# The feed-forward stage's second matrix in seven half-size products, with weight sums made by accumulating DMAs

## The chip, the core and the metric

The kernel runs on one NeuronCore of a Trainium2 chip. Its time is device microseconds of the whole program, the median of three runs. TensorE (PE) multiplies matrices, ScalarE (ACT), VectorE (DVE) and GpSimd (POOL) work on tiles in SBUF, and SyncE (SP) only issues DMAs.

## The reference, cut to what matters

The program is a model of two blocks on 512 tokens of width 1024 in fp32. Attention layers, a memory and a pooling layer come first; the change leaves them alone. The last stage is a feed-forward network (FFN) and a last norm:

```python
hm = rms_norm(x, g_mlp[l])                                    # (512, 1024)
x = x + jnp.square(jax.nn.relu(hm @ w_up[l])) @ w_down[l]     # (1024, 4096), (4096, 1024)
return rms_norm(x, g_final)
```

`jnp.square(relu(...))` is called ff below. "Up" is the product with `w_up`, "down" the one with `w_down`.

## The kernel before, in words

Every product of fp32 matrices is made of three matmuls of rounded parts (`mm3`, L376 to L378): each operand is split into a high part `hi` (rounded by ACT) and the rest `lo` (a DVE subtraction), and hi·hi, hi·lo and lo·hi are summed in PSUM. Weights come from HBM in slabs of 1 MB (8 x 256 or 4 x 512 columns a partition, tile `wraw`), by DMAs on SP's queue. `split_slab` makes `whi` (ACT, L208) and `wlo` (DVE, L209) of them in four pieces of 512 columns. Two raw slabs and two split slabs are resident at a time.

The program is a list of units, each of which emits one product and may return a "post", the work on its result, which is emitted behind the next unit. `emit` walks the list, and behind each unit it emits pieces of coming splits and the loads of slabs whose buffers are free. So the order of every engine's queue is fixed when the program is built; at run time each engine takes its queue in order and waits on semaphores.

The FFN goes in four chunks of 1024 hidden columns. `up(c)` makes 8 products 128x512 of 24 matmuls each (8 k x 3) from four slabs; its post takes relu (ACT), the square (DVE) and splits it into tiles `ffgh` and `ffgl` (L392, L393), which are double-buffered. `down(c)` goes over two halves of 512 output columns; in each, four blocks of 128 tokens (`tb`) take 24 matmuls 128x512 (8 k x 3) from two slabs; the post adds the PSUM tile to `x` (DVE, L1873). `x` is eight tiles, `xs[tb][half]`. Two products of `up(c+1)` are emitted ahead of `down(c)`, the other six behind it.

In the last down the second half goes block by block, and `last(tb)` is emitted as soon as a block is complete: the sum of squares of its second half (ACT into `junk`, L438), v^-0.5 by a polynomial in small DVE instructions (L442, L443, L402 to L408), the final gain (POOL, L1898), the scaling (ACT L1899 and DVE L1900, one half each) and two DMAs out. The first halves' sums of squares were made before. POOL does nothing else in the FFN but issue the two loads of the final gain (L432).

Of the kernel before, what the change touches and what calls it, by code (L numbers as in the profile page):

```python
# [26 lines left out]
def block_kernel(ctx: ExitStack, tc: tile.TileContext, A: dict, out: bass.AP, stop=None):  # L27
# [40 lines left out]
    class Pool:  # L68
        """a pool opened and closed by units of the program"""
# [50 lines left out]
    def load_constants():  # L120
        """rows of small vectors, to be transposed to columns; the loads are issued a few at a time"""
# [60 lines left out]
    # ---------------------------------------------------------------- weights: slabs of up to 2112 columns a partition  # L182
# [8 lines left out]
    def dma_slab(key):  # L191
# [5 lines left out]
        raws[key] = t  # L197

    def split_slab(key):
        """hi and lo parts of a slab, in pieces to be emitted one after the other"""  # L200
# [42 lines left out]
    def weave(steps, main, lead=0):  # L243
        """(units before, units after) of each step, with main's units (but the first lead) spread evenly between the two"""
        res, m = main[:lead], 0
        main = main[lead:]
        for i, (before, after) in enumerate(steps):
            to = (len(main) * (i + 1)) // len(steps)
            res += before + main[m:to] + after
            m = to  # L250
        return res

    def soft_steps(scores, norms, trans, values, per, deep=1):
        """steps of an attention: scores of step i, normalization of step i-1 and transposes of the step deep before;
        values of a head after its last transposes"""
# [18 lines left out]
    n = {"dma": 0, "split": 0, "freed": 0, "limit": 0, "start": 2, "step": 2}  # L274
    order = []

    def dma_first(i):
        dma_slab(order[i])
        n["dma"] = i + 1

    def emit():
# [6 lines left out]

        todo = []
# [10 lines left out]

        def pump():
            while n["limit"]:
                if n["split"] < min(n["dma"], n["limit"]) and n["split"] - n["freed"] < NB and not todo:
# [4 lines left out]
                elif n["dma"] < len(order) and n["dma"] - n["split"] < NRAW:  # L308
                    dma_slab(order[n["dma"]])
# [8 lines left out]
        def flush():  # L318
            """a slab's next piece, the second parts of posts, the posts; slabs no more needed are freed"""
            while pend:  # L320
# [12 lines left out]
                for k in prog[i][1]:  # L333
                    if last[k] == i:
                        ready.pop(k)
                        n["freed"] += 1
                pump()

        for i, (fn, keys, early, quiet) in enumerate(prog):
# [9 lines left out]
            for k in keys:  # L349
                if k not in ready:  # L350
                    pieces(order[n["split"] - 1])
                    pump()
                assert k in ready, ("slab not resident", k)
# [8 lines left out]
    def rate(start, step):  # L362
        """pieces of a slab that are split at once, and after a product"""
# [9 lines left out]
    # ---------------------------------------------------------------- helpers  # L373
# [24 lines left out]
    def newton(v, n, eng=None):  # L398
        """v ** -0.5 of [128, n]: from the halved exponent, by a polynomial in v y y"""
# [12 lines left out]
        # the same polynomial as a product of two quadratic ones  # L412
# [13 lines left out]
    # ---------------------------------------------------------------- norms  # L426
# [27 lines left out]
    def norm_T(st, tb, h, dst):  # L454
        """half h of a normed block to columns tb of its transpose; dst(h) gives the tiles of that half"""
# [16 lines left out]
    # ---------------------------------------------------------------- products: units  # L472
# [17 lines left out]
    def fm_halves(items, src="xt"):  # L490
        """(key, c0, post): the first 256 tokens of each, then the rest"""
# [15 lines left out]
    def outproj(name, w, row, nk, slots=(0, 1), blockwise=True):  # L507
        """units of x += y w[128 row...] from slots of y, two parts of 128 rows each"""
# [25 lines left out]
    def boundary(op, mid={}, fa=(), fb=(), gain=False):  # L534
        """the last product into x (block by block), its norm and transpose, and units that run meanwhile"""
# [48 lines left out]
    def mem_kv_units(layer, mt):  # L584
        """keys (normed, transposed) and values of the memory attention into S['mk'], S['mv']"""
# [60 lines left out]
    # ---------------------------------------------------------------- softmax over 256 keys  # L646
# [29 lines left out]
    # ---------------------------------------------------------------- memory attention  # L676
# [79 lines left out]
    # ================================================================ block 1, layer A  # L756
# [20 lines left out]
    def keep_mt():  # L777
        """the normed memory, transposed, for the second layer"""
# [92 lines left out]
    def head_units(h):  # L871
        """z, o, v, q, k of a head"""
# [151 lines left out]
    # h3: tile, z (4), o (2), v (2), q (2), k (2)  # L1024
# [67 lines left out]
    # ================================================================ block 1, layer B  # L1092
# [140 lines left out]
    # ---- heads  # L1233
# [158 lines left out]
    def pt_view(i, j):  # L1392
        """block j of the queries against blocks 0..j of the keys, each 384 columns after the last"""
# [31 lines left out]
    # ================================================================ block 2: pooling and differential attention  # L1425
# [162 lines left out]
    def dprep(h):  # L1588
        """q and k of a head, turned"""
# [19 lines left out]
    def dattend(h):  # L1609
        sc, no, tr, pv = [], [], [], []  # L1610
        for j in range(4):
            def f1(j=j):
# [5 lines left out]
                # the two parts take turns: they hold different rows of the array  # L1618
# [15 lines left out]
            def f2(j=j):  # L1634
                # e0 + (-lambda s0 / s1) e1; the factor 1 / s0 is left to the norm
# [59 lines left out]
    def dsteps():  # L1695
        """steps of the four heads: scores of step i, normalization and transposes of step i-1, values of step i-2"""
# [3 lines left out]
        for i in range(21):  # L1700
# [9 lines left out]
            # after the values of a head's last block: the sums, the products, the transposes  # L1710
# [19 lines left out]
    # y of the pooled part has to be used before that of head 0 is written  # L1730
# [22 lines left out]
    # ================================================================ block 2: cross attention  # L1753
# [81 lines left out]
    def open_ff():  # L1835
# [3 lines left out]
        ffp.open()  # L1839

    def up(c):
        res = []
        for s in range(4):
            key = cslab(("up", c, s), w_up, 1024 * c + 256 * s, 256)
            for i in range(2):
                def post(ps, f_=2 * s + i):
                    if f_ == 0:
                        C["ff", c] = pair(ffp.p, [128, 8, 512], "ffg", bufs=2)
                    g = C["ff", c]
                    r = T("r")  # L1850
                    act.activation(out=r, in_=ps, func=AF.Relu)  # L1851
                    dve.tensor_tensor(out=r, in0=r, in1=ps, op=ALU.mult)  # L1852
                    split(g[0][:, f_, :], g[1][:, f_, :], r)

                res.append((key, 128 * i, post))
        return res

    def down(c):
        res = []
        for half in range(2):  # L1860
            for s in range(2):
                key = cslab(("dn", c, half, s), w_down, 512 * half, 512, k0=8 * c + 4 * s, nk=4)
                for tb in range(4):
                    def fn(w, half=half, s=s, tb=tb):
                        g = C["ff", c]
                        if s == 0:
                            C["dn", tb] = bank([128, 512], "dn")
                        ps = C["dn", tb]
                        t = slice(tb * 128, tb * 128 + 128)
# [5 lines left out]
                    res.append(U(fn, key))  # L1875
# [7 lines left out]
    ups = [up(c) for c in range(4)]  # L1883
    uf, ur = fm_halves(ups[0][0:4])
# [88 lines left out]
```

## Time and profile before

| what | value |
|---|---|
| median of three runs | 1642.2 us (1641.59 to 1644.99) |
| profiled execution, span | 1641.7 us, 0.5 us under that median |
| PE busy in the span | 1581.1 us (96%), 8809 matmuls |
| DVE, ACT, POOL busy | 959.0, 684.2, 148.1 us |
| FFN with its last norm | from about 1296 us to the end |

The span is that of one profiled execution. PE's busy time is the sum of what its matmuls take, weight loads (PEld) run beside them. A row of the timeline gives an instruction's start and its own duration, both in us; what lies between the starts of two matmuls divided by the number of steps is called the pitch below.

### The profile page before, as it was taken

To read this page: it belongs to the slowest core of one execution; us is meant where nothing else is said; L and a number is where in the kernel's file an instruction comes from. 1 tells how busy PE (TensorE), PEld (TensorE's weight loads), DVE (VectorE), ACT (ScalarE), POOL (GpSimd) and SP (SyncE) were. 2 spreads that over 40 slices of the span, in tenths; PEclk is the share of its full clock that TensorE was granted. 3 is DMA by queue.
4 is the path that set the end of the run, shared out by engine and by line. 5 is a ranking of instruction groups with operands and counts; after the bars stand their busy time and mean duration, and the time that the engine had idled before them with its cause. 6 is when DMAs were issued, how large, how long until landed. Compare 5 with 4: busy or idle time off the path is not lost.

```text
span 1641.7 us, 22734 instructions
## 1 busy us (share of the span) xinstructions
PE 1581.1 (96%) x8809; PEld 1342.8 (82%) x8809; DVE 959.0 (58%) x1977; ACT 684.2 (42%) x1491; POOL 148.1 (9%) x471
## 2 busy tenths in 40 slices
PE   6999999999999999999989999998999999999997
PEld 6889898988788978778879877777987888888886
DVE  6558647565685563667776657567357543434345
ACT  6344424333464543444554434455334432323232
POOL 4100000000030000111211000012001000000002
PEclk9999999999999999999999999999999999999999
DMA  8322223132242221212415332224221233223221
GB/s 273 129 78 78 78 82 99 52 103 77 103 136 77 71 78 59 67 35 66 155 39 180 98 101 78 78 90 141 78 78 52 78 103 103 90 90 116 90 90 52
DMA packets 126149, 152.65 MB, mean 93 GB/s; under 512 B 7169, under 2 KB 103193, under 8 KB 126041
## 3 DMA queue, kind: packets, MB, share of 16 engines
q1 hardware_dynamic: 123736, 144.63, 27.5%
q0 software_dynamic: 2304, 6.57, 1.4%
q8 instruction: 69, 1.13, 0.3%
q14 instruction: 40, 0.32, 0.1%
HBM read 144.88 MB, written 6.31 MB: 92 GB/s over the span
## 4 chain that ended last, share of the span: by engine, by line
PE 43%; DVE 4%; ACT 2%; issue 1%; POOL 0%; ACTq 0%; DVEq 0%; POOLq 0%
PE fm L377 7%; PE fm L378 7%; PE fm L376 7%; PE dn L376 4%; PE dn L378 4%; PE dn L377 4%; PE op L377 1%; PE op L378 1%; PE op L376 1%; DVE wlo L209 1%; PE sc L1624 0%; PE ck L377 0%; ACT junk L438 0%; PE ck L378 0%; PE ck L376 0%
## 5 line engine op out<-in xcount | busy, mean ns | idle before, releaser
L377 PE MATMUL fm<-xtl,whi 128*128 128x512 f32 (+1 forms) x888 | 332.3, 374 | 1.5 <-DVE xtl L393 1.5
L376 PE MATMUL fm<-xth,whi 128*128 128x512 f32 (+1 forms) x888 | 332.4, 374 | 0.2 <-ACT xth L392 0.2
L378 PE MATMUL fm<-xth,wlo 128*128 128x512 f32 (+1 forms) x888 | 332.6, 375 | 0.0
L209 DVE TENSOR_TENSOR wlo<-wraw,whi 128x512 fp32r<-128x512 f32 (+2 forms) x436 | 276.8, 683 | 87.2 <-ACT whi L208 77.3
L208 ACT ACTIVATE whi<-wraw 128x512 fp32r<-128x512 f32 (+2 forms) x436 | 244.0, 618 | 156.3 <-PE dn L378 89.2
L377 PEld LDWEIGHTS fm<-xtl,whi 128*128 128x128 f32 x888 | 169.1, 190 | 33.0 <-DVE xtl L393 2.5
L376 PEld LDWEIGHTS fm<-xth,whi 128*128 128x128 f32 x888 | 169.0, 190 | 30.3 <-ACT xth L392 0.7
L378 PEld LDWEIGHTS fm<-xth,wlo 128*128 128x128 f32 x888 | 169.2, 191 | 29.2
L376 PE MATMUL tm<-whi,xth 128*128 128x256 f32 x416 | 116.6, 280 | 0.0
L377 PE MATMUL tm<-wlo,xth 128*128 128x256 f32 x416 | 116.0, 279 | 0.0
L378 PE MATMUL tm<-whi,xtl 128*128 128x256 f32 x416 | 115.9, 279 | 0.0
L525 DVE TENSOR_TENSOR x<-op,x 128x512 f32<-128x512 f32 x120 | 81.7, 686 | 47.4 <-PE op L378 47.2
L376 PE MATMUL dn<-whi,ffgh 128*128 128x512 f32 x256 | 101.5, 397 | 0.0
L378 PE MATMUL dn<-whi,ffgl 128*128 128x512 f32 x256 | 101.4, 396 | 0.0
L377 PE MATMUL dn<-wlo,ffgh 128*128 128x512 f32 x256 | 101.1, 395 | 0.0
L403 POOL TENSOR_TENSOR rsx<-rsy 128x1 f32<-128x1 f32 (+2 forms) x49 | 15.0, 305 | 753.6 <-DVE rsy L402 707.3
L376 PEld LDWEIGHTS tm<-whi,xth 128*128 128x128 f32 x416 | 78.9, 190 | 0.2
L378 PEld LDWEIGHTS tm<-whi,xtl 128*128 128x128 f32 x416 | 79.0, 190 | 0.0
L377 PEld LDWEIGHTS tm<-wlo,xth 128*128 128x128 f32 x416 | 78.8, 189 | 0.2
L376 PE MATMUL op<-whi,y0h 128*128 128x512 f32 x160 | 66.8, 417 | 0.0
L1852 DVE TENSOR_TENSOR r<-r,fm 128x512 f32<-128x512 f32 x32 | 22.0, 687 | 74.0 <-ACT r L1851 74.0
L377 PE MATMUL op<-wlo,y0h 128*128 128x512 f32 x160 | 63.7, 398 | 0.0
(537 smaller groups left out, 3250.5 us busy)
## 6 DMA issues: line engine op xcount, KB each, us to landing
wraw<-in_a_w_in_dram SPq DMA_DIRECT2D x23, 1024.0 KB
wraw<-in_w_up_dram SPq DMA_DIRECT2D x16, 1024.0 KB
wraw<-in_w_down_dram SPq DMA_DIRECT2D x16, 1024.0 KB
wraw<-in_mem_w_kv_dram SPq DMA_DIRECT2D x8, 1024.0 KB
wraw<-in_b_w_in_dram SPq DMA_DIRECT2D x8, 1024.0 KB
wraw<-in_w_ckv_dram SPq DMA_DIRECT2D x8, 1024.0 KB
wraw<-in_w_in_dram SPq DMA_DIRECT2D x8, 1024.0 KB
wraw<-in_a_w_out_dram SPq DMA_DIRECT2D x6, 1024.0 KB
```

Source lines behind the costliest of these rows:

```text
L208: act.activation(out=hi[:, s], in_=t[:, s], func=AF.Copy)
L209: dve.tensor_tensor(out=lo[:, s], in0=t[:, s], in1=f(hi)[:, s], op=ALU.subtract)
L376: pe.matmul(out=ps, lhsT=lh, rhs=rh, start=first, stop=False)
L377: pe.matmul(out=ps, lhsT=lh, rhs=rl, start=False, stop=False)
L378: pe.matmul(out=ps, lhsT=ll, rhs=rh, start=False, stop=last)
L403: eng.tensor_tensor(out=x, in0=y, in1=y, op=ALU.mult)
L525: return lambda: dve.tensor_tensor(out=xs[tb][h], in0=ps, in1=xs[tb][h], op=ALU.add)
L1852: dve.tensor_tensor(out=r, in0=r, in1=ps, op=ALU.mult)
```

## The change

Only the FFN changes. `x` becomes one tile `xall` (four token blocks of 1024 columns), the same bytes in another shape.

Each chunk's down product is done half by half as a 2x2 block product: tokens in two halves of 256, hidden columns in two interleaved halves of 512 (`i`), output columns in two of 256 (`j`). Instead of eight block products it takes seven (Winograd's variant of Strassen's scheme): seven combinations of the ff blocks, seven of the weight blocks, and sums of the results. A block product is 2 token blocks x 4 k x 3 = 24 matmuls 128x256. The instructions go from 768 matmuls 128x512 to 8 groups x 7 x 24 = 1344 matmuls 128x256.

- **Weights** come in blocks of 1024 columns (512 KB). Of a group's four, three (U, V, W) are loaded raw by SP. The other combinations are made in place by 32 accumulating DMAs from POOL's queue, four a group (three from HBM, one from SBUF): block order U, V, W, U+b01, V+b01, then U+b11, then W+U. Each is issued once the split of the buffer's last state is done. Split blocks live in a ring of six slots: the four halves of the two old slabs' tiles, and two old `y` tiles. The split of a block needs the slot of the sixth block before it.
- **ff side**: `keep_ff` keeps seven operands of 256 tokens instead of two of 256; four POOL subtractions or additions 128x256 per 256 hidden columns make the four sums, ACT and DVE split them. ff is single-buffered, so the first two results of the next chunk are kept back until `down(c)` is done.
- **up** of chunks 1 to 3 runs in blocks of half of K (4 k), and the first two blocks of these (s = 0) stand ahead of `down(c)`, as many products as before.
- **Results**: a product is added into up to two blocks of x, and two products go through an SBUF copy (`pc` by ACT, `pu` by DVE). Of 12 sums in a half nine are on DVE and three on POOL (all on DVE in the very last half).
- **Tail**: with `SEVEN = (0, 6, 1, 3, 4, 5, 2)` the quarters x[0][1] and x[1][1] of the last half are complete after the sixth product, x[1][0] after the seventh. `last(0)` and `last(1)` are emitted around the seventh product, `last(2)` and `last(3)` behind it.

```diff
-    xs = [[const.tile([128, 512], F32, name=f"x{tb}{h}") for h in range(2)] for tb in range(4)]
+    xall = const.tile([128, 4, DM], F32, name="xall")
+    xs = [[xall[:, tb, h * 512:h * 512 + 512] for h in range(2)] for tb in range(4)]
...
+    def wgroup(name, b):
+        for n_, src, uses in (("U", b[0][0], 4), ("V", b[1][1], 2), ("W", b[1][0], 2)):
+            bufs[name, n_] = {"src": src, "at": None, "step": None, "uses": uses}
+        steps = (("U", 0, ("U", b[0][1])), ("V", 0, ("V", b[0][1])), ("W", 0, None), ("U", 1, ("U", b[1][1])),
+                 ("V", 1, ("W", "U")), ("U", 2, None), ("W", 1, None))
...
+    def split_block(key):
...
+        def piece():
+            act.activation(out=hi, in_=b["at"], func=AF.Copy)
+            dve.tensor_tensor(out=lo, in0=b["at"], in1=f(hi), op=ALU.subtract)
+
+        def after():
...
+                if isinstance(nxt[1], str):
+                    o = bufs[name, nxt[1]]
+                    pool.dma_start(out=v4(d["at"]), in_=v4(o["at"]), accum_op=ALU.add)
+                    raw_done(o)
+                else:
+                    pool.dma_start(out=v4(d["at"]), in_=nxt[1], accum_op=ALU.add)
...
+    def keep_ff(f_, r):
...
+        put(1, 2, r)
+        sa, sb = T("sa"), T("sb")
+        pool.tensor_tensor(out=sa[:, t0], in0=r0[:, t1], in1=r[:, t1], op=ALU.subtract)
+        pool.tensor_tensor(out=sa[:, t1], in0=r0[:, t0], in1=r0[:, t1], op=ALU.subtract)
+        put(3, 2, sa)
+        pool.tensor_tensor(out=sb[:, t0], in0=sa[:, t0], in1=r0[:, t0], op=ALU.subtract)
+        pool.tensor_tensor(out=sb[:, t1], in0=r[:, t0], in1=sb[:, t0], op=ALU.add)
+        put(5, 2, sb)
...
     def down(c):
...
-                        for k in range(4):
-                            mm3(ps, (g[0][:, 4 * s + k, t], g[1][:, 4 * s + k, t]), (w[0][:, k, :], w[1][:, k, :]),
-                                s == 0 and k == 0, s == 1 and k == 3)
-                        return (lambda: dve.tensor_tensor(out=xs[tb][half], in0=ps, in1=xs[tb][half], op=ALU.add)) if s else None
...
+            def post(i, ps, x=x, tmp=tmp, eng=dve if final else pool):
+                if i == 0:
+                    tmp["t"] = v2(T("pc"))
+                    act.copy(out=tmp["t"], in_=ps)
+                    plus(eng, x[0][0], tmp["t"])
+                elif i == 1:
+                    plus(dve, x[0][1], ps)
+                elif i == 2:
+                    plus(dve, x[0][0], ps)
+                elif i == 3:
+                    plus(dve, x[0][1], ps)
+                    plus(dve, x[1][1], ps)
+                elif i == 4:
+                    plus(dve, x[1][0], ps)
+                    plus(dve, x[1][1], ps, op=ALU.subtract)
+                elif i == 5:
+                    u = v2(T("pu"))
+                    dve.tensor_tensor(out=u, in0=ps, in1=tmp["t"], op=ALU.add)
+                    plus(eng, x[0][1], u, op=ALU.subtract)
+                    plus(dve, x[1][0], u)
+                    plus(eng, x[1][1], u, op=ALU.subtract)
+                else:
+                    plus(dve, x[1][0], ps)
...
+                    for k in ks:
+                        mm3(ps[:, tb, :], (gh[:, op, k, t], gl[:, op, k, t]), (w[0][:, k, :], w[1][:, k, :]), tb == 0 and k == 0, tb == 1 and k == 3)
...
-    for c in range(1, 4):
-        u_ = [fmu(*v_) for v_ in ups[c]]
-        add(u_[0:2], down(c - 1), u_[2:])
+    for c in range(3):
+        u_ = up_blocks(c + 1)
+        add(u_[0:4], down(c), U(lambda: [keep_ff(f_, C.pop(("r", f_))) for f_ in range(2)]), u_[4:])
     d = down(3)
...
-    for tb in range(4):
-        add(d[8 + tb], d[12 + tb], U(lambda tb=tb: last(tb)))
+    stats = [U(lambda tb=tb: norm_half(sts[tb], xs[tb][0], 0)) for tb in range(4)]
+    add(U(last_gain), d[0:-14], d[-14:-10], stats[0:2], d[-10:-8], stats[2:4], d[-8:-2], U(lambda: last(0)), d[-2:-1], U(lambda: last(1)),
+        d[-1:], U(lambda: last(2)), U(lambda: last(3)))
```

POOL's queue in one chunk after the change, from the last ff sums of the chunk to the first down half's and the second half's work. L249 is an accumulating DMA from HBM into a raw block, L246 the one from SBUF, L2004 to L2008 are the ff sums, L2030 the sums into x.

```order
L2004 TENSOR_TENSOR sa<-r 128x256
L2005 TENSOR_TENSOR sa<-r 128x256
L2007 TENSOR_TENSOR sb<-sa,r 128x256
L2008 TENSOR_TENSOR sb<-r,sb 128x256
L249 DMA wraw<-in_w_down_dram 128x4x256
L246 DMA wraw<-wraw 128x1024
L2030 TENSOR_TENSOR xall<-xall,pc 128x2x256
L249 DMA wraw<-in_w_down_dram 128x4x256 x3
L2030 TENSOR_TENSOR xall<-xall,pu 128x2x256 x2
L246 DMA wraw<-wraw 128x1024
```

Before, POOL's queue had none of these rows. The second half's first three accumulating DMAs stand between two kinds of sums into x, and its last one behind them.

DVE's queue in one half of a down before the change, the halves' four sums behind two slabs' splits:

```order
L209 TENSOR_TENSOR wlo<-wraw,whi 128x512 x8
L1873 TENSOR_TENSOR x_81<-dn,x_81 128x512
L1873 TENSOR_TENSOR x_83<-dn,x_83 128x512
L1873 TENSOR_TENSOR x_85<-dn,x_85 128x512
L1873 TENSOR_TENSOR x_87<-dn,x_87 128x512
```

DVE's queue in a half of a down after it; L236 is the split of a block of 1024 columns, L2030 a sum into x, L2049 the sum `pu`.

```order
L2030 TENSOR_TENSOR xall<-xall,dn 128x2x256
L236 TENSOR_TENSOR wl<-wraw,wh 128x1024
L2030 TENSOR_TENSOR xall<-xall,dn 128x2x256
L236 TENSOR_TENSOR wl<-wraw,wh 128x1024
L2030 TENSOR_TENSOR xall<-xall,dn 128x2x256 x2
L236 TENSOR_TENSOR wlo<-wraw,whi 128x1024
L2030 TENSOR_TENSOR xall<-xall,dn 128x2x256 x2
L236 TENSOR_TENSOR wlo<-wraw,whi 128x1024
L2049 TENSOR_TENSOR pu<-dn,pc 128x512
L2030 TENSOR_TENSOR xall<-xall,pu 128x2x256
L236 TENSOR_TENSOR wlo<-wraw,whi 128x1024
L2030 TENSOR_TENSOR xall<-xall,dn 128x2x256
```

A half's DVE sums grew from four to nine, and they now alternate with the splits of weight blocks.

ACT's last rows before the change; the `fs` names are the sums of squares of the four token blocks, `rst` their factors:

```order
L208 ACTIVATE whi<-wraw 128x512
L438 ACTIVATE junk,fs_14748<-x_84 128x512
L438 ACTIVATE junk,fs_14749<-x_86 128x512
L438 ACTIVATE junk,fs_14746<-x_81 128x512
L1899 ACTIVATE x_80<-x_80,rst_14918 128x512
L438 ACTIVATE junk,fs_14747<-x_83 128x512
L1899 ACTIVATE x_82<-x_82,rst_14964 128x512
```

ACT's last rows after the change:

```order
L546 ACTIVATE junk,fs_15330<-xall 128x512
L546 ACTIVATE junk,fs_15327<-xall 128x512
L2104 ACTIVATE xall<-xall,rst_15719 128x512
L546 ACTIVATE junk,fs_15328<-xall 128x512
L2104 ACTIVATE xall<-xall,rst_15752 128x512
L546 ACTIVATE junk,fs_15329<-xall 128x512
L2104 ACTIVATE xall<-xall,rst_15785 128x512
```

The order on ACT is as before: a block's sum of squares, then its scaling, then the next block's. What has moved is the product whose results they read.

## Rows read from the trace of the kernel before

**Rows 1.** The page: span, and busy time of each engine (share, instructions).

```profile
span 1641.7 us, 22734 instructions
...
PE 1581.1 (96%) x8809; PEld 1342.8 (82%) x8809; DVE 959.0 (58%) x1977; ACT 684.2 (42%) x1491; POOL 148.1 (9%) x471
```

**Rows 2.** Stretches: length, busy PE, PEld, DVE, ACT, POOL, PE clock, DMA, GB/s.

```profile
1296.00:1632.00 336.00, 335.75 (x1446) 271.35 (x1444) 142.65 (x239) 105.11 (x192) 10.04 (x9) 1.00 0.29 93
...
1345.40:1349.40 4.00, 4.00 (x19) 3.29 (x18) 0.69 (x1) 0.00 (x0) 0.00 (x0) 1.00 0.82 262
```

**Rows 3.** Timeline of PE in the FFN: first matmuls of quarters; the last matmul.

```profile
1330.07 0.39 PE L376 MATMUL dn<-whi,ffgh 128*128 128x512 f32 x1
...
1374.03 0.39 PE L376 MATMUL fm<-xth,whi 128*128 128x512 f32 x1
...
1418.82 0.40 PE L376 MATMUL dn<-whi,ffgh 128*128 128x512 f32 x1
...
1463.62 0.40 PE L376 MATMUL fm<-xth,whi 128*128 128x512 f32 x1
...
1586.79 0.40 PE L376 MATMUL dn<-whi,ffgh 128*128 128x512 f32 x1
...
1631.36 0.39 PE L378 MATMUL dn<-whi,ffgl 128*128 128x512 f32 x1
```

**Rows 4.** Timeline of PE in an earlier stage: 15 matmuls 128x256, first and last.

```profile
376.14 0.28 PE L378 MATMUL tm<-whi,xtl 128*128 128x256 f32 x1
...
377.73 0.28 PE L377 MATMUL tm<-wlo,xth 128*128 128x256 f32 x1
```

**Rows 5.** Timeline of a slab's split, four pieces in a row.

```profile
1352.24 2.20 ACT L208 ACTIVATE whi<-wraw 128x512 fp32r<-128x512 f32 x4 [8.74 <-PE dn L378]
...
1352.91 2.50 DVE L209 TENSOR_TENSOR wlo<-wraw,whi 128x512 fp32r<-128x512 f32 x4
```

**Rows 6.** DMA issues on POOL's queue: count, KB each, median us to landing.

```profile
rkb<-rd POOLq DMA_DIRECT2D x8, 256.0 KB, 4.9
...
cs<-in_c_rope_dram POOLq DMA_DIRECT2D x1, 512.0 KB, 3.6
```

**Rows 7.** The tile rkb: the spread of its DMAs.

```profile
DMA to landing us min/median/max: 4.4/4.9/7.8
```

**Rows 8.** Groups by line, 1400 us to the end: busy, mean ns, idle before.

```profile
L1873 DVE TENSOR_TENSOR x<-dn,x 128x512 f32<-128x512 f32 x24 | 16.6, 690 | 34.0 <-PE dn L378 34.0
...
L1898 POOL TENSOR_TENSOR x<-x,gain 128x512 f32<-128x512 f32 x8 | 10.2, 1288 | 112.1 <-ACT junk L438 112.1
...
L403 DVE TENSOR_TENSOR rsx<-rsy 128x1 f32<-128x1 f32 x4 | 3.8, 962 | 0.1
...
L408 DVE TENSOR_SCALAR rst<-rst,rsx 128x1 f32<-128x1 f32 x8 | 1.7, 214 | 0.3
```

**Rows 9.** Timeline behind the last matmul: DVE, ACT and POOL.

```profile
1631.79 0.69 DVE L1873 TENSOR_TENSOR x<-dn,x 128x512 f32<-128x512 f32 x1 [0.85 <-PE dn L378]
...
1633.71 0.94 DVE L403 TENSOR_TENSOR rsx<-rsy 128x1 f32<-128x1 f32 x1
...
1632.57 0.63 ACT L438 ACTIVATE junk<-x 128x512 f32<-128x512 f32 x1 [1.42 <-DVE nv L442]
...
1635.99 0.72 ACT L1899 ACTIVATE x<-x,rst 128x512 f32<-128x512 f32 x1 [2.69 <-DVE rst L408]
...
1633.37 1.26 POOL L1898 TENSOR_TENSOR x<-x,gain 128x512 f32<-128x512 f32 x1 [3.06 <-ACT junk L438]
```

**Rows 10.** Timeline of POOL: the issue of one DMA.

```profile
1506.28 0.59 POOL L432 DMA_DIRECT2D gain<-in_g_final_dram  x1 [228.24 <-DVE ffgl L393]
```

More of the change, by code (lines that the diff above doesn't have):

```diff
@@ L272, in soft_steps @@
         return res
-    n = {"dma": 0, "split": 0, "freed": 0, "limit": 0, "start": 2, "step": 2}
-    order = []
+    n = {"dma": 0, "split": 0, "freed": 0, "limit": 0, "start": 2, "step": 2, "y": 0, "ring": 0, "raw": 0}
+    order, loads = [], []
     def dma_first(i):
-        dma_slab(order[i])
+        dma_raw(loads[i])
         n["dma"] = i + 1
@@ L287, in emit @@
                 last[k] = i
+        slabs_n = sum(k not in blocks for k in order)
+        for k in order:
+            r = blocks[k][0] if k in blocks else k
+            if r not in loads:
+                loads.append(r)
         todo = []
@@ L307, in pump @@
                     pieces(count=n["start"])
-                elif n["dma"] < len(order) and n["dma"] - n["split"] < NRAW:
-                    dma_slab(order[n["dma"]])
+                elif can_load():
+                    r = loads[n["dma"]]
+                    if r in bufs:
+                        b = bufs[r]
+                        b["at"], b["step"] = free_raw.pop(0), 0
+                        nc.sync.dma_start(out=v4(b["at"]), in_=b["src"])
+                    else:
+                        dma_raw(r)
                     n["dma"] += 1
@@ L349, in emit @@
             for k in keys:
-                if k not in ready:
+                while k not in ready:
+                    before = n["split"]
                     pieces(order[n["split"] - 1])
                     pump()
+                    assert n["split"] > before, ("no place for", k)
                 assert k in ready, ("slab not resident", k)
@@ L1839, in open_ff, with up_post, post @@
         ffp.open()
+        n["y"] = 2
+    def up_post(c, f_):
+        def post(ps):
+            r = T("r")
+            act.activation(out=r, in_=ps, func=AF.Relu)
+            dve.tensor_tensor(out=r, in0=r, in1=ps, op=ALU.mult)
+            if c and f_ < 2:
+                C["r", f_] = r
+            else:
+                keep_ff(f_, r)
+        return post
     def up(c):
+        return [(cslab(("up", c, s), w_up, 1024 * c + 256 * s, 256), 128 * i, up_post(c, 2 * s + i)) for s in range(4) for i in range(2)]
@@ L1842, in up, with up_blocks @@
+    def up_blocks(c):
         res = []
         for s in range(4):
[L1844 to L1855, printed above, removed]
@@ new lines, in up_blocks, with put @@
+        return res
+    def keep_ff(f_, r):
+        s_ = f_ // 2
+        if f_ == 0:
+            if "ff" not in C:
+                C["ff"] = pair(ffp.p, [128, 7, 4, 256], "ffg")
+            C["r0"] = r
+        gh, gl = C["ff"]
+        def put(o, n_, src):
+            split(gh[:, o:o + n_, s_, :], gl[:, o:o + n_, s_, :], src.rearrange("p (a b) -> p a b", a=n_))
+        if f_ % 2 == 0:
+            C["r0"] = r
+            put(0, 1, r[:, 0:256])
+            return
+        r0, (t0, t1) = C.pop("r0"), (slice(0, 256), slice(256, 512))
+        put(1, 2, r)
[6 more added lines that the diff above has]
+        put(5, 2, sb)
@@ L1858, in down @@
+    SEVEN = (0, 6, 1, 3, 4, 5, 2)
     def down(c):
@@ new lines, in down, with v2, plus @@
+            keys = wgroup(("dn", c, half), [[src[:, i, :, 512 * half + 256 * j:512 * half + 256 * j + 256] for j in range(2)] for i in range(2)])
+            x = [[xall[:, 2 * i:2 * i + 2, 512 * half + 256 * j:512 * half + 256 * j + 256] for j in range(2)] for i in range(2)]
+            tmp = {}
+            final = c == 3 and half == 1
+            def v2(t):
+                return t.rearrange("p (a b) -> p a b", a=2)
+            def plus(eng, dst, src, op=ALU.add):
+                eng.tensor_tensor(out=dst, in0=dst, in1=src, op=op)
@@ L1876, in down, with both @@
+            def both(i, ks):
+                return [part(i, tb, ks) for tb in range(2)]
+            ks = list(range(4))
+            if c == 3 and half == 0:
+                res += both(0, ks[0:3]) + both(1, ks[0:3]) + both(0, ks[3:]) + both(2, ks) + both(1, ks[3:])
+            else:
+                res += both(0, ks) + both(1, ks) + both(2, ks)
+            for i in range(3, 7):
+                res += both(i, ks)
         return res
@@ L1881, in next_xt_ff @@
         S["gain"] = gain_tiles(A["g_mlp_2"], cap.p)
-    ups = [up(c) for c in range(4)]
-    uf, ur = fm_halves(ups[0][0:4])
-    add(U(next_xt_ff), boundary(oc1, fa=uf, gain=True), U(open_ff), ur, [fmu(*u_) for u_ in ups[0][4:]])
+    ups = up(0)
+    uf, ur = fm_halves(ups[0:4])
+    add(U(next_xt_ff), boundary(oc1, fa=uf, gain=True), U(open_ff), ur, [fmu(*u_) for u_ in ups[4:]])
     fin = {}
```

101 lines of the change are left out of this document (86 added, 15 removed).

## The prediction

> **What bounds the kernel now.** I read the page first: PE is busy in 96% of the span [rows 1]. The stretches of the stage that changes say the same more sharply: from 1296 to 1632 us PE is busy for 335.75 of 336 us at full granted clock, DVE for 142.65, ACT for 105.11, POOL for 10, and the DMA engines work at 0.29 of their time [rows 2]. Nothing waits for weights. So time can be won here only by taking work off PE, or lost by making PE wait, or behind the last matmul, where 10.34 us pass (1631.36 to 1641.7) [rows 1, 3].
>
> Down's present cost is read from the starts of matmuls. A quarter of it is 192 matmuls. The first takes 1374.03 − 1330.07 = 43.96 us, the second 1463.62 − 1418.82 = 44.80 [rows 3], a pitch of 0.229 and 0.233 us. The last goes from 1586.79 to 1631.36 for 191 steps, 0.2334. With the third like the second, down costs 43.96 + 3 x 44.80 = 178.4 us.
>
> **PE's saving.** 1344 matmuls 128x256 replace 768 of 128x512. The same shape, a block of tokens held and 256 weight columns moved, runs in an earlier stage: 14 steps in 1.59 us, 0.1136 [rows 4]. Bounds: 0.1136 from that row gives 152.7 us, a saving of 25.7. Half of the slower 512 pitch, 0.1167, gives 156.8 and 21.5. The rise from the first quarter to the later ones (2%) may come over the 256 form too, and short forms may pay more at product borders; 0.120 gives 161.3 and 17. I take 23, between the first two, because the 256 row is the same shape but a short stretch. Up keeps its matmuls: blocks of half K are 12 matmuls on the same bank, in the same number.
>
> **The tail.** It is longer, since the norm can no longer go block by block under the matmuls. Before, the sum of block 3 starts 0.43 us behind the last matmul's start, the sum of squares at 1632.57, the scaling at 1635.99, 3.42 later, and the end comes 5.71 behind that [rows 1, 9]. The first three norms are done by then.
>
> Afterwards all four norms need a result of product 6 of 7. Call the start of its last matmul q. DVE makes `pu` at q + 0.43, takes it from x[0][1] (0.69 each, [rows 8]), and ACT's first sum of squares starts at q + 1.81. ACT's queue then alternates sum of squares and scaling, and the scaling needs DVE's factor, so the norms run one behind the other: 3.42 from sum of squares to scaling, 0.72 for the scaling [rows 9], four times over, without the last scaling: 4 x 3.42 + 3 x 0.72 = 15.84. Two sums into x ahead of the first norm on DVE cost 0.4, since only what outlasts ACT's 0.63 counts; the sum of product 7 stands in DVE's queue behind the second norm and makes the third wait 0.5 to 0.6. The last scaling starts at q + 1.81 + 15.84 + 1.0 = q + 18.65 and the end is at q + 24.4. Product 7 (24 x 0.1136 = 2.73) lies under that, so 21.6 us pass behind the last matmul's start, against 10.3: +11.3. Bounds: 9 if the small DVE instructions are shorter when POOL leaves them alone (below), 13 if POOL's gains of two blocks meet.
>
> Sum: 1641.7 − 23 + 11.3 + 1 (half a dozen borders between halves and chunks at 0.1 to 0.2) = 1631.0. The median of before is 0.5 above the profiled time; that is inside the rounding.
>
> **What hides the rest, and what it costs without cover.** The split of a block takes ACT 1.1 and DVE 1.25 us (half of 2.20 and 2.50, [rows 5]), the pair 2.4 in series. Seven a half are 7.7 on ACT and 8.75 on DVE, in the 19.1 us of a half's matmuls. Nine DVE sums of 0.69 make DVE 15.0 of 19.1 us, three POOL sums (1.29 each, [rows 8]) 3.9. The ff sums on POOL are 16 a chunk of about 0.65 (half of 1.29), 10 us beside up's 88. Issuing an accumulating DMA occupies POOL for about 0.59 [rows 10]. All that is covered.
>
> The real question is the chain of weight sums, which the trace doesn't show. Let *a* be the time from the issue of an accumulating DMA to its landing. In the second half of a chunk all happens while PE multiplies without up work between. The first block's slot comes free with the end of the second product of the half before, 5.45 us into it; its split ends at 8.0 (1.1 + 1.25 and a handover); then U + b01 (a), the split of that (2.45), U + b11 (a), W + U (a), the split (2.4). The product that reads it starts at 19.1 + 6 x 2.73 = 35.5. So 8.0 + 2.45 + 2.4 + 3a ≤ 35.5, or a ≤ 7.5; in the last chunk the slots come 2 us later, a ≤ 6.8. In first halves the chain starts under up's matmuls and bears a = 11. Beyond these PE stalls by 3 x 3 (a − 7.5) + 3 (a − 6.8).
>
> The nearest rows: 512 KB by a POOL DMA land 3.6 us after the issue [rows 6]. An accumulating one has to read 512 KB of destination too; at 262 GB/s, the rate of a stretch in which the queues are at work [rows 2], that is 2.0 more: 5.6. I take 6. The low bound is 3.6, the high one the slowest POOL DMA shown, 7.8 for 256 KB [rows 7], plus 2.0: about 10. In POOL's queue an L249 that waits for a split keeps the sums behind it waiting, and x[0][0] for those; nobody on PE waits for these sums but the tail, and there they are on DVE.
>
> A rule of the Trainium skill speaks against this value: by "DMA: Bandwidth & Descriptors", section "Measured (HBM→SBUF, 128 partitions, SWDGE, issued from GpSimd)", a DMA of 1 MB issued from GpSimd takes 6.15 us of transfer alone. If an accumulate of 512 KB counts as 1 MB moved, that is an estimate of 7.9 with 1.7 of setup (3.6 less 512 KB at 262 GB/s), and the sum would be 1638. No row of this trace shows an accumulate, so it can't be weighed further.
>
> **Rivals.**
>
> *The chain is a little too long (a = 7.9).* POOL DMAs of 256 KB land 4.9 us after the issue in the median [rows 6]. From there, 256 KB more at 262 GB/s are 1.0 and the reading of 512 KB of destination 2.0: a = 7.9. PE stalls by 9 x 0.4 + 3 x 1.1 = 7 us: 1638. For it: eight DMAs stand behind that median, one behind the 3.6. Against: the one is of the right size, and its source is HBM as here.
>
> *The chain is far too long: slower.* Place: the last two products of every second half. PE stands before the block W + U, whose three DMAs come one after the other. The gain of 11 is gone at a = 8.3 (9 x 0.8 + 3 x 1.5 = 11.7), and a = 10 costs 9 x 2.5 + 3 x 3.2 = 32: 1663. For it: 7.8 has been seen for half the bytes, and blocks come in rows of 256 columns, 1 KB pieces. Against: medians of 3.6 and 4.9.
>
> *DVE becomes the bound.* In the tail a DVE instruction on 128x1 with two SBUF inputs takes 0.94 when a POOL instruction of 1.26 that started 0.34 before it runs, and ends when that one ends (1634.63 and 1634.65) [rows 9]; its neighbours with one tile and a scalar take 0.21 [rows 8]. So such a DVE instruction waits for POOL's to end. The Trainium skill states that mechanism: by "SBUF — State Buffer", section "Who interferes with whom", a DVE instruction with two SBUF inputs and a GpSimd one that reads SBUF lock each other out for a whole instruction; these two rows agree. Three POOL sums of 1.29 a half would bring DVE from 15.0 to 18.9 of 19.1 us; with the issue of DMAs or ff sums beside it, it could reach 21: 8 halves x 2 = 16 less, 1647, or no change if only half of the halves suffer. For it also: the splits, half of DVE's work, have two SBUF inputs. Against: sums from PSUM have one, so not every collision counts, and PE has up to six split blocks ahead.
>
> *More is gained.* PE keeps 0.1136 and the tail's small instructions run at 0.21 to 0.3 where POOL is still busy elsewhere: 25.7 − 9, 1625.
>
> *The work isn't taken away* (PE's time for a short matmul hardly under that for a long one): excluded by [rows 4].
>
> **Chances and range.** The forecast, chain hidden, 1631 (own range 1626 to 1636): 0.55. The chain a little too long, 1638: 0.11. Much too long: 0.17, spread over 1640 to 1665. DVE bound: 0.09, 1636 to 1650. More gain, 1622 to 1626: 0.08. A difference of 0.2%, 3.3 us, is about what a measurement of this kernel can tell from no change. Faster by more than that (under 1638.9): 0.55 + 0.08 + 0.06 + 0.02 = 0.71, rounded down to 0.68 as the chain isn't shown anywhere. Same (1638.9 to 1645.5): 0.12; slower: 0.20. The range leaves out a tenth at either end: 1623 to 1654.
>
> **What the profile after would show.** PE's pitch of the 256 matmuls at 0.114 to 0.120 without idle time between: right on the saving. A wait of PE before the last two products of second halves, released by the split of W + U or U + b11, with landings over 7.5 us: the chain. Landings of 5 to 7 and no wait: right. The distance from the last matmul's start to the end: 21.6. DVE's busy time in a down half near 15 of 19 us, with splits far over 1.25 us: the lock. Wrong altogether if PE idles at the start of a down, where ff's operands come from POOL through a queue that holds waiting DMAs; then the place of a DMA issue in POOL's order would be the cause, which I priced at nothing because two up blocks (11 us) stand ahead of each down.

## The result and the profile after

The changed kernel takes 1670.2 us (median of four, 1666.2 to 1671.6) against 1643.6: ratio 1.0159, 95% interval 1.0143 to 1.0176. It is slower; 1631 was forecast. The profiled execution has a span of 1669.0 us, 27.3 above that of before. The page of the changed kernel, the lines that answer to [rows 1], and its DMAs from POOL:

```profile
span 1669.0 us, 24268 instructions
...
PE 1572.0 (94%) x9385; PEld 1364.0 (82%) x9385; DVE 1044.7 (63%) x2020; ACT 721.1 (43%) x1499; POOL 285.9 (17%) x588
...
wraw<-in_w_down_dram POOLq DMA_DIRECT2D x24, 512.0 KB, 6.3
```

PE is busy 9 us less, and its share of the span has fallen from 96% to 94%. Where it waited, by the view of waits from 1320 us to the end (total us, times, longest):

```profile
PE dn L484 <- ACT ffgh L500: 7.5, 2, 5.9
PE dn L485 <- DVE wlo L236: 6.9, 7, 1.9
PE dn L485 <- DVE wl L236: 4.3, 5, 2.1
PE dn L484 <- ACT whi L235: 2.9, 2, 1.8
PE dn L484 <- ACT wh L235: 1.3, 1, 1.3
```

All waits are in down, all but the first group for splits of weight blocks. From the starts of matmuls, as in [rows 3], the 27.3 us come apart so:

| part | before | after | difference |
|---|---|---|---|
| to the first down matmul | 1330.07 | 1333.51 | +3.4 |
| four downs | 178.1 | 47.05 + 47.60 + 45.04 + 50.83 = 190.5 | +12.4 |
| up between them | 123.2 | 122.4 | -0.8 |
| last matmul's start to the end | 10.3 | 22.6 | +12.2 |

Of the first line, 1.1 us come at the start of the stage, 0.8 of them a new wait for a slab's split; 2.3 arose ahead of it, in code that the change leaves alone, and differ from run to run (profiles of the same instructions of these runs lay from 1.7 earlier to 3.4 later than before at 1284 us). Of down's 190.5 us, 158.0 are what the 1344 matmuls take when nothing waits (the run e1_no_sums below), 27.0 are gaps between matmuls beyond one normal step, and 5.4 are 56 matmuls that start further apart than usual. Of these, 40 (3.8 us), nearly all 0.213 apart in place of 0.1176, stand in three rows, each behind gaps, and the stretches (columns as in [rows 2]) show the granted clock there:

```profile
1469.40:1472.60 3.20, 3.20 (x18) 3.20 (x17) 3.20 (x5) 1.61 (x2) 0.00 (x0) 0.51 0.77 230
1601.60:1606.10 4.50, 4.49 (x23) 4.32 (x24) 1.80 (x3) 1.08 (x2) 0.00 (x0) 0.62 1.02 205
1446.00:1457.00 11.00, 11.00 (x96) 11.00 (x95) 8.31 (x10) 2.15 (x3) 4.33 (x5) 1.00 0.71 114
```

In the first the clock is 0.51, its lower level of 1.2 GHz; the second, at 0.62, is at the lower level for most of its length; in the third, without gaps, it is 1.00. Not every gap is followed by such a row: the one of 2.3 us at 1366.3 in the first chunk, the longest there, is not.

**Where the gaps come from** is read from the chain that ended last. It is shown for the second chunk, whose down runs from 1425.07 to 1472.67 (start, length, what the chain goes through; "issue" is time in which nothing that the profile shows was waited for):

```profile
1428.16 7.94 DMA wraw<-in_w_down_dram
1437.74 1.85 POOL xall L2030
1439.59 5.71 issue
1445.31 6.04 DMA wraw<-in_w_down_dram
1454.58 5.84 DMA wraw<-in_w_down_dram
1460.71 5.27 DMA wraw<-wraw
```

Two chains of weight sums run one behind the other: the end of the first half's from 1428.16, then the second half's three accumulates from 1445.31. The second starts 20.2 us into the down. Why, ACT's timeline says (start, duration, instruction, idle before and its releaser):

```profile
1425.02 0.63 ACT L500 ACTIVATE ffgh<-sb 128x512 fp32r<-128x512 f32 x1 [1.35 <-POOL sb L2008]
1425.55 1.99 ACT L235 ACTIVATE whi<-wraw 128x1024 fp32r<-128x1024 f32 x2
...
1436.13 1.06 ACT L235 ACTIVATE whi<-wraw 128x1024 fp32r<-128x1024 f32 x1 [7.61 <-DMA wraw<-in_w_down_dram]
...
1440.96 2.01 ACT L235 ACTIVATE wh<-wraw 128x1024 fp32r<-128x1024 f32 x2 [3.30 <-DMA wraw<-wraw]
...
1451.46 1.06 ACT L235 ACTIVATE whi<-wraw 128x1024 fp32r<-128x1024 f32 x1 [5.43 <-DMA wraw<-in_w_down_dram]
...
1460.52 1.06 ACT L235 ACTIVATE wh<-wraw 128x1024 fp32r<-128x1024 f32 x1 [5.08 <-DMA wraw<-in_w_down_dram]
...
1466.06 1.06 ACT L235 ACTIVATE wh<-wraw 128x1024 fp32r<-128x1024 f32 x1 [4.00 <-DMA wraw<-wraw]
```

ACT takes its queue in order. The split of U + b01 stands behind the last ff split (1425.02), so U + b11 is issued 3.1 us into the down. The split of W + U waits for its landing until 1440.96. The second half's first block, raw and asked for some 34 us before (at 1407.39), is the other of the two splits in that row. It stood behind a wait it had nothing to do with.

### The profile page after: what moved, and what is told of

It reads as the page before. It is cut to its first block, busy times and chain, and to the rows that moved or that the text cites. A ratio compares the mean times of both kernels' runs of the same rounds, so it can differ in the third digit from the quotient of the medians.

```text
span 1669.0 us, 24268 instructions
## 1 busy us (share of the span) xinstructions
PE 1572.0 (94%) x9385; PEld 1364.0 (82%) x9385; DVE 1044.7 (63%) x2020; ACT 721.1 (43%) x1499; POOL 285.9 (17%) x588
## 4 chain that ended last, share of the span: by engine, by line
PE 25%; issue 6%; DVE 6%; DMA 6%; POOL 4%; ACT 3%; ACTq 0%; POOLq 0%; DVEq 0%; SPq 0%
DMA wraw<-in_w_down_dram 5%; PE fm L485 4%; PE fm L484 4%; PE fm L486 4%; PE op L485 1%; PE op L486 1%; PE op L484 1%; DMA wraw<-wraw 1%; POOL xall L2030 1%; DVE wlo L267 1%; POOL sb L2008 1%; POOL sa L2005 1%; DVE wlo L236 1%; ACT junk L546 1%; POOL sa L2004 1%
## 5 line engine op out<-in xcount | busy, mean ns | idle before, releaser
L485 PE MATMUL fm<-xtl,whi 128*128 128x512 f32 (+1 forms) x824 | 306.9, 372 | 1.5 <-DVE xtl L501 1.5
L486 PE MATMUL fm<-xth,wlo 128*128 128x512 f32 (+1 forms) x824 | 306.9, 372 | 0.1
L267 DVE TENSOR_TENSOR wlo<-wraw,whi 128x512 fp32r<-128x512 f32 (+2 forms) x324 | 206.1, 679 | 33.0 <-ACT whi L266 23.3
L266 ACT ACTIVATE whi<-wraw 128x512 fp32r<-128x512 f32 (+2 forms) x324 | 182.5, 619 | 38.7 <-PE op L486 23.1
L633 DVE TENSOR_TENSOR xall<-op,xall 128x512 f32<-128x512 f32 x120 | 81.6, 686 | 47.4 <-PE op L486 47.3
L236 DVE TENSOR_TENSOR wlo<-wraw,whi 128x1024 fp32r<-128x1024 f32 x53 | 75.1, 1425 | 47.9 <-ACT whi L235 47.9
L485 PE MATMUL dn<-wlo,ffgh 128*128 128x256 f32 x296 | 84.4, 285 | 6.9 <-DVE wlo L236 6.9
L235 ACT ACTIVATE whi<-wraw 128x1024 fp32r<-128x1024 f32 x53 | 54.7, 1052 | 78.8 <-DMA wraw<-in_w_down_dram 49.6
L484 PE MATMUL dn<-whi,ffgh 128*128 128x256 f32 x296 | 84.0, 284 | 2.9 <-ACT whi L235 2.9
L486 PE MATMUL dn<-whi,ffgl 128*128 128x256 f32 x296 | 83.7, 283 | 0.0
```

The lines of the kernel that those rows point to most:

```text
L235: act.activation(out=hi, in_=b["at"], func=AF.Copy)
L236: dve.tensor_tensor(out=lo, in0=b["at"], in1=f(hi), op=ALU.subtract)
L266: act.activation(out=hi[:, s], in_=t[:, s], func=AF.Copy)
L267: dve.tensor_tensor(out=lo[:, s], in0=t[:, s], in1=f(hi)[:, s], op=ALU.subtract)
L484: pe.matmul(out=ps, lhsT=lh, rhs=rh, start=first, stop=False)
L485: pe.matmul(out=ps, lhsT=lh, rhs=rl, start=False, stop=False)
```

## The experiments

**The floor.** e1_no_sums takes the accumulating DMAs out, so that the blocks of the sums hold raw blocks.

```diff
-                    pool.dma_start(out=v4(d["at"]), in_=v4(o["at"]), accum_op=ALU.add)
+                    pass
...
-                    pool.dma_start(out=v4(d["at"]), in_=nxt[1], accum_op=ALU.add)
+                    pass
```

> Leaves out all 32 accumulating DMAs, so the weight blocks of the sums hold the raw blocks; everything else as after the change. Theory A (PE waits for the chain of weight sums, and in the last chunk for ff sums that stand behind a waiting DMA in POOL's queue; the clock falls in these waits): of 27 us of gaps in down and some 5 us of matmuls at half clock nearly all go: 1636 to 1640. Theory B (short matmuls, DVE and POOL are the limit whatever the DMAs do): 1655 or more.

Measured: 1633.5 us, 0.9933 of before (0.9918 to 0.9948); span 1630.8. The four downs take 39.53, 39.51, 39.53 and 39.42 us without one gap, and 20.9 us pass behind the last matmul's start. That is theory A, 2.5 us under its range. It is also what the forecast comes to without the sums: 158.0 us of matmuls at a pitch of 0.1176 save 20.1, and the tail takes 10.6 of that back. One such down:

```profile
1413.60:1453.00 39.40, 39.40 (x337) 39.40 (x336) 30.36 (x32) 16.33 (x17) 8.40 (x6) 1.00 0.43 132
```

DVE is busy for 77% of it and doesn't limit it.

**The ff sums.** e2_ff_dve writes `dve` for `pool` in the four instructions of `keep_ff`.

> The four ff sums of a pair (sa, sb) on DVE in place of POOL. Theory A: the 6.2 us wait for ff in the last chunk goes, and ACT and DVE, which stood between POOL's sums, reach the split of U+b01 some 3 us sooner in each chunk, so that the chain starts sooner: 1650 to 1660. A rival (only the landing time of the accumulates counts, not what stands ahead of the splits): only the 6.2 us and the clock behind it, 1661 to 1663. DVE as the limit: no gain or a loss.

Measured: 1672.3 us (1.0172, 1.0155 to 1.0190): no gain. The accumulates' times say why: U + b11 of the second chunk is issued 2.3 us into its down (1428.18 against 1425.84), nearly as before. PE's waits for ff in the last chunk fall from 7.5 us to 3.1, but its second half, which had none, now has 4.1 us of gaps for weight blocks, and the first and third downs are some 2 us longer than in the changed kernel, the second 2.6 shorter. My account of how the chain starts was wrong in this: the chain did not start sooner when another engine did the ff sums. That the ff work's place ahead of the splits is what counts fits this, but no run moved it.

**The sums into x.** e3_x_dve replaces `eng=dve if final else pool` by `eng=dve`.

> The three sums into x of a half that POOL made are made by DVE. Theory C (POOL's sums hold DVE's split of a block for up to 4.05 us in place of 1.22, and that split lies on the chain): 2.8 us less in each of four second halves, 1658 to 1662. Theory A alone: 1666 to 1670, since the chain of the half before sets when the second begins. DVE as the limit: slower.

Measured: 1658.8 us (1.0085, 1.0070 to 1.0101). The number is that of theory C, its reason only in part. In the changed kernel DVE's split of one block a second half is slow beside two POOL sums; first DVE's row, then POOL's:

```profile
1455.48 4.05 DVE L236 TENSOR_TENSOR wlo<-wraw,whi 128x1024 fp32r<-128x1024 f32 x1 [0.37 <-ACT whi L235]
```

```profile
1455.36 3.08 POOL L2030 TENSOR_TENSOR xall<-xall,pu 128x512 f32<-128x512 f32 x2
```

PE's gap of 2.1 us at 1457.4 waits for this block, and without POOL's sums it is gone. But the three accumulates of the second chunk's second half are as far apart as before (9.3 and 6.6 us, against 9.3 and 6.1). They begin 14.6 us into the down in place of 20.2: POOL comes to that chunk's ff sums sooner (1369.3 in place of 1390.5), and U + b11 is issued 2.5 us ahead of the down in place of 3.1 behind its start. The slow split itself moved and did not vanish: POOL's ff sums, now sooner, run beside the last block's split, and PE has gaps of 3.1 us behind it in the first and the third chunk.

```profile
1369.62 3.17 DVE L236 TENSOR_TENSOR wlo<-wraw,whi 128x1024 fp32r<-128x1024 f32 x1 [3.49 <-ACT whi L235]
```

```profile
1369.28 1.07 POOL L2004 TENSOR_TENSOR sa<-r 128x256 f32<-128x256 f32 x1
```

**The tail.** e4_plain_last computes the very last half without the seven products, one block of 128 tokens after the other, with 192 matmuls 128x256 in place of 168 and only the two sums b00 + b10 and b01 + b11.

```diff
+        terms = {0: ((0, 0, 1, 2), (0, 1, 1, 3)), 1: ((3, 0, 2, 4), (3, 1, 2, 5))}
+        for tb in range(4):
+            ps_ = {}
+            for j in range(2):
+                o0, k0, o1, k1 = terms[tb // 2][j]
...
+    for tb in range(4):
+        add(d_[4 * tb:4 * tb + 4], U(lambda tb=tb: last(tb)))
```

> The very last half without the seven products: 192 matmuls 128x256 (against 168), block of tokens by block of tokens, with two weight sums that don't follow one another, and the norm of a block right behind its last matmul. If the tail is what I take it for (22.6 us behind the last matmul's start since all four norms wait for the sixth product): 10 to 11 us behind the last matmul, 2.8 us more matmuls: 1658 to 1661. If the tail is long for another reason (DVE or POOL busy with other things): 1665 or more.

Measured: 1659.1 us (1.0092, 1.0075 to 1.0109). 8.9 us pass behind the last matmul's start (1651.3 to 1660.2) in place of 22.6. So the order of the norms was the tail. In the changed kernel ACT's rows, where [rows 9] had one pair, show four norms, one behind the other:

```profile
1647.08 0.63 ACT L546 ACTIVATE junk<-xall 128x512 f32<-128x512 f32 x1 [3.33 <-DVE xall L2030]
...
1651.88 0.72 ACT L2104 ACTIVATE xall<-xall,rst 128x512 f32<-128x512 f32 x1 [4.08 <-DVE rst L516]
1652.51 0.61 ACT L546 ACTIVATE junk<-xall 128x512 f32<-128x512 f32 x1
...
1655.91 0.72 ACT L2104 ACTIVATE xall<-xall,rst 128x512 f32<-128x512 f32 x1 [2.69 <-DVE rst L516]
...
1660.51 0.72 ACT L2104 ACTIVATE xall<-xall,rst 128x512 f32<-128x512 f32 x1 [2.69 <-DVE rst L516]
...
1664.54 0.72 ACT L2104 ACTIVATE xall<-xall,rst 128x512 f32<-128x512 f32 x1 [2.69 <-DVE rst L516]
```

e8_xdve_plain joins this and e3_x_dve.

> Both of e3_x_dve (all sums into x on DVE) and e4_plain_last. If the gains (11 and 9 us) are separate: 1648 to 1651. If DVE, which takes the sums and the last half's splits, gets too busy, or the gains are one and the same: 1655 or more.

Measured: 1648.3 us (1.0030, 1.0017 to 1.0044): the gains add.

**The landing time.** e7_plain_dma drops `accum_op=ALU.add` from both DMAs, so that the sums are not made and a block holds what was moved into it last.

> The 32 accumulating DMAs become plain DMAs at the same places of the same bytes, so the sums are not made (they hold the block added last). If the landing time of an accumulate is what makes the chain too long: landings of about 4 in place of 6.3 us, a chain 6 to 7 us shorter in each half, 1640 to 1650. If the splits' place in the order of ACT and DVE sets when the chain starts, whatever it takes: 1658 or more.

Measured: 1636.5 us (0.9957, 0.9942 to 0.9973), 3.5 under the expected range, and no gap in any down. The landings of the DMAs from HBM, of the changed kernel and then of this one:

```profile
L249 POOL DMA_DIRECT2D wraw<-in_w_down_dram x24: 1274/1300/1618, 1324.5 to 1628.7; - x24
...
DMA to landing us min/median/max: 5.8/6.3/8.5
```

```profile
L249 POOL DMA_DIRECT2D wraw<-in_w_down_dram x24: 748/766/836, 1325.5 to 1597.8; - x24
...
DMA to landing us min/median/max: 4.3/4.6/5.5
```

Those from SBUF take 4.6 and 3.6. A half's three DMAs are thus 4.4 us shorter (2 x 1.7 + 1.0), and issuing one from HBM takes POOL 0.77 us in place of 1.30. In the second chunk the second half's chain also starts 12.9 us into the down (1431.54 against 1418.61), 7.3 sooner, since the first half's chain ahead of it is shorter and begins sooner too (U + b11 at 1418.89, 0.3 us into the down in place of 3.1). So a shorter landing counts twice, once in each of two chains that follow one another. It also shows that the late start is a cause only together with landings of this length: with the order left as it is, shorter DMAs alone remove every gap.

**The order of the splits.** e9_order puts one key at another place of the list of splits and changes nothing else.

```diff
+        for c in range(4):
+            a, b = (("dn", c, 0), 3), (("dn", c, 1), 0)
+            if b in order:
+                order.remove(b)
+                order.insert(order.index(a) + 1, b)
```

> Only the order of the splits changes: the first block of a chunk's second half is split right behind U+b01 of the first half, ahead of W+U of the first half, in place of behind it; the sums, products and engines are as after the change. Theory Q (the second half's chain starts late, some 20 us into the down in place of 8, because its first split stands in ACT's queue behind a split that waits for the landing of the first half's last sum): its first accumulate is issued 3 to 8 us into the down, the gaps of second halves (some 13 us and the clock behind them) go, 1650 to 1657. If the length of one half's chain is what is too long, whenever it starts: 1664 or more.

Measured: 1652.1 us (1.0046, 1.0031 to 1.0060), 18 us under the changed kernel with the same DMAs, whose landings are no shorter (6.2 us from HBM and 6.0 from SBUF in the median). The gaps in second halves fall from 16.1 us to 4.0. POOL's timeline shows the second half's first accumulate issued right behind the first half's U + b11, 3 to 4 us into the down (which starts at 1419.81):

```profile
1422.83 2.62 POOL L249 DMA_DIRECT2D wraw<-in_w_down_dram  x2 [3.18 <-DVE wl L236]
1428.96 0.89 POOL L246 DMA_DIRECT2D wraw<-wraw  x1 [3.52 <-DMA wraw<-in_w_down_dram]
```

This tells theory Q from the rival: the length of one half's chain is, but for those 4 us, bearable if it starts in time.

e10_order_xdve_plain takes this, all sums into x on DVE and the plain last half.

> The order of e9_order, all sums into x on DVE, the very last half without the seven products. If the causes add: what is left are the first halves' gaps (about 1 us each), the wait for ff sums in the last chunk (4 to 6 us) and the start: 1632 to 1640, faster than before. If the early split only moves the wait to the next half: 1645 or more.

Measured: 1634.6 us (0.9934, 0.9914 to 0.9954). The downs of the second and the third chunk have no gap; PE still waits 3.3 us for ff in the last. In the changed kernel that wait was 5.9 us, and POOL's rows show why: the ff sums stand behind an accumulate that waits for another's landing.

```profile
1608.11 0.89 POOL L246 DMA_DIRECT2D wraw<-wraw  x1 [6.93 <-DMA wraw<-in_w_down_dram]
1608.68 1.06 POOL L2004 TENSOR_TENSOR sa<-r 128x256 f32<-128x256 f32 x1
```

e11_all_inside gives these last sums alone to DVE.

```diff
-                keep_ff(f_, r)
+                keep_ff(f_, r, dve if c == 3 and f_ >= 6 else pool)
```

> As e10_order_xdve_plain, and the last chunk's last ff sums are made by DVE in place of POOL, where they stood behind an accumulating DMA that waits for another to land (3.6 us of gap in e10_order_xdve_plain, and half clock behind it). If that wait is a cause of its own: 4 to 6 us less, 1628 to 1631. If DVE, which then holds splits and sums before the same product, takes as long: 1633 to 1636.

Measured: 1628.7 us (0.9902, 0.9882 to 0.9922). PE's only wait in down is left in the first chunk:

```profile
PE dn L490 <- DVE wlo L236: 0.8, 1, 0.8
```

**The sums elsewhere.** e5_dram makes them in HBM, spread over the stages before, and the FFN loads plain blocks.

```diff
+            keys = [wblock(("dn", c, half, n_), s_) for n_, s_ in enumerate((b[0][0], b[1][1], b[1][0], t["U1"], t["V1"], t["U2"], t["W1"]))]
...
+            return lambda: nc.sync.dma_start(out=summed[g][1][k], in_=summed[g][0][i][j])
...
+            return lambda: pool.dma_start(out=summed[g][1][k], in_=summed[g][1][o] if isinstance(o, str) else summed[g][0][o[0]][o[1]], accum_op=ALU.add)
```

> The four weight sums of each group are made in HBM during the earlier stages (32 copies on SP's queue, 32 accumulating DMAs on POOL's, spread over them); the feed-forward stage loads seven plain blocks a group and has no accumulating DMA. Everything else as after the change. Theory A (the chain of sums inside the stage is what PE waits for): as with the sums left out, 1630 to 1635. Rival D (the extra DMAs delay the loads or POOL's small instructions of earlier stages): the feed-forward stage is as short, but starts late, 1640 or more.

Measured: 1638.8 us (0.9970, 0.9957 to 0.9983), 4 above the expected range. The FFN is that of e1_no_sums to 0.02 us a down. The rest lies ahead of it: the first down matmul comes at 1334.0 against 1329.5 there. Whether the 64 extra DMAs cost that or the early stages' own spread did, these runs don't settle; e7_plain_dma, which has none of the extra DMAs, came to it at 1334.6.

e6_dram_plain adds the plain last half.

> The same, and the very last half without the seven products, block of tokens by block of tokens as in the run e4_plain_last. If tail and chain are separate causes: 9 us under the run e5_dram, 1621 to 1626, faster than before the change by about 1%. If the last half's six resident blocks come too late: 1628 to 1635.

Measured: 1628.4 us (0.9907, 0.9892 to 0.9922), 2 above the expected range, and so inside that of its rival, blocks that come too late. The trace speaks against the rival: PE has no wait in any down, the last takes 42.24 us as in e11_all_inside, and what is over lies ahead of the stage, as in e5_dram (first down matmul at 1334.5). With e11_all_inside it is the fastest version, 0.9% to 1% under the kernel before.

## Why the prediction was wrong

The profile is 38 us above the forecast of 1631.0: 32.5 are gaps and slow matmuls in down, which the forecast had at nothing, 2.9 are missing from PE's saving, 0.9 are the tail and 3.4 the time to the first down matmul, less 0.8 in up and the 1 us for borders.

- *What bounds the kernel*: right. Both fast versions come back to PE without gaps, but for 0.8 us of waits in e11_all_inside.
- *PE's saving of 23*: 20.1 when nothing waits, so the term was 3 too large. The pitch is 0.1176, inside the bounds 0.1136 to 0.120, nearer to half of the 512 pitch than I took. The stretch of [rows 4] was too short to stand for its stage: of the steps of its matmuls in the kernel before, some 840 are 0.113 or 0.114, as there, but some 330 are 0.117 to 0.119.
- *The tail, +11.3*: right, +12.2 (and +10.6 in e1_no_sums). e4_plain_last showed the cause. The 1 us for borders wasn't there: in a down of e1_no_sums no step is over 0.120.
- *The length of a*: right. I took 6; the three landings of a chain are 6.3, 6.3 and 4.6 in the median. Splits and handovers included, the second half's chain runs from 1445.31 to the end of its last split at 1468.4, 23.1 us, where 3 x 6 + 2.45 + 2.4 = 22.9 were forecast. From the 1 MB row of the Trainium skill's "DMA: Bandwidth & Descriptors" (section "Measured (HBM→SBUF, 128 partitions, SWDGE, issued from GpSimd)") I had an estimate of 7.9 if an accumulate of 512 KB counts as 1 MB moved. The measured 6.3 decides against that reading; the row itself, of a plain DMA of 1 MB, no run here tests.
- *The step that failed* is the start of that chain: "The first block's slot comes free with the end of the second product of the half before, 5.45 us into it; its split ends at 8.0". The slot may be free then. The split stands in ACT's queue behind the split of W + U of the first half, and is done 20 us into the down (second chunk). With 20.2 in place of 8.0, 35.5 − 20.2 − 4.85 leaves 10.4 us for three landings, 3.5 each, and no accumulate in these runs is as short (4.5 the least). e9_order moved that one split in each chunk and took back 18 of the 32 us of gaps and slow matmuls. The rival "The chain is far too long" had the place right, the last two products of second halves, but its reason was an *a* of 8 to 10; here landings of 6.3 did it, since the chain began late.
- *"In first halves the chain starts under up's matmuls and bears a = 11"*: wrong in the same way. U + b11 was issued 3.1 us into the down, behind the ff splits, and the last block of a first half was some 1.1 us late in two chunks. I had asked when buffers come free and not what stands ahead in each queue.
- *The place of a DMA issue in POOL's queue, priced at nothing*: a wait of 5.9 us in the last chunk, which has no up blocks ahead of its down. The text had named it as what would make it wrong. It and the chain cover for each other: most of it removed alone (e2_ff_dve, where 3.1 us of waits for ff stay) gave nothing, removed with the chain mended (e10_order_xdve_plain to e11_all_inside) 5.9.
- *DVE as the bound*: not in sum (77%), but the lock is real: a split, with two inputs in SBUF, took 4.05 us in place of 1.22 and ended 1.1 behind the 3.08 us of POOL's two sums. By the Trainium skill's "SBUF — State Buffer" (section "Who interferes with whom") such a DVE instruction contends with a GpSimd one that reads SBUF; these rows agree. It cost 1.4 to 2.3 us in each of three second halves, where it fell on a block that PE needed next.
- *What I left out*: some gaps cost more than themselves, since the matmuls behind them ran at the lower clock (0.5): 3.8 of the 5.4 us of matmuls that start further apart.

Not settled: why the ff work runs one pair late against PE all through up, which seems to set how late the first half's chain is. Giving its sums to DVE changed U + b11's place in the second chunk by 0.8 us; giving POOL's x sums to DVE by 5.6.

## What to carry to other kernels

Ask of each step in a prefetch chain not only when its buffer is free, but what stands ahead of it in the queue of every engine that it passes, and whether that waits for a DMA; one split in each chunk moved ahead of such a wait was worth 18 us here. A chain of DMAs that each need the last one's landing must start in time or be shorter, and two chains in one in-order queue add up. When several waits cover for one another, mend them together before you call one of them harmless.

## What the runs showed that I had not expected

- An accumulating DMA of 512 KB takes 1.30 us of POOL to issue and 6.3 us to land; the same DMA without adding takes 0.77 and 4.6 (e7_plain_dma). From SBUF to SBUF it is 0.89 and 4.6 against 0.56 and 3.6.
- POOL's sums of 128x256 mostly took, by turns, about 0.74 and 1.20 us, where I had halved 1.29.
